# Second layer norm of a decoder layer: root and bias of five row tiles through TensorE instead of VectorE

## The chip, the cores and the metric

The kernel runs on one core of a Trainium2 chip. The metric is device time in microseconds (us) from launch to end; lower is better. The median of the runs shown is 1836.4 us. The profile's clock starts at the first instruction of the span, and all times of rows below are on that clock.

## What is computed

The kernel is a whole decoder layer on 2048 rows of 1024 float32 channels: a mixer of two branches, a first layer norm, a mixture of SwiGLU experts and a second layer norm. Only the end matters here:

```
h   = layer_norm(ALPHA * x + mix, ln1_g, ln1_b)
moe = hier_moe(h, ...)
out = layer_norm(ALPHA * h + moe, ln2_g, ln2_b)

layer_norm(x, g, b): mu = mean(x); var = mean((x - mu)^2)
                     return (x - mu) * rsqrt(var + 1e-5) * g + b
```

## The kernel before

The experts (L1520 to L1553) add their rows into the DRAM tensor `acc`, which also holds ALPHA times h. After the last expert the second norm begins (from L1584). Its 2048 rows are 16 tiles of 128 rows by 1024 channels, grouped in six units `F[k]` of 2, 2, 4, 2, 4 and 2 tiles. A tile is called (k, t) below: (4, 2) is tile 2 of unit 4. SyncE's queue loads every unit from `acc` at L1590, in order.

Four steps make the norm of a unit:

- the moments: for units 1, 2, 4 and 5 on ScalarE (`moments`, L1610), two passes per tile; for units 0 and 3 on VectorE (`moments_v`, L1599).
- `scale1` (L1629): on VectorE, one instruction per tile, f = (f - mean) * g. The vector g lies in PSUM as `g2p`.
- `root` (L1637): on VectorE, rsqrt by a first guess and three Newton steps, 11 small instructions on [128, n] columns named `f_v`, `f_rs` and `f_q`. `f_rs` holds the roots.
- `scale2` (L1651): on VectorE, one instruction per tile, f = f * rs + b, with b in PSUM as `b2p` (L1662). When a pair of tiles, or a tile that stands alone, is done, SyncE's queue stores it to `out` (L1664).

One tile in each of the units 1 to 4, (1, 1), (2, 3), (3, 1) and (4, 3), is left out of `scale1` and `scale2` and normed on GpSimd (POOL) by three instructions of its own once the roots are there: L1657, L1658 and L1659, with g and b in SBUF (`eraw`). It stores that tile itself (L1660).

The order on each engine is the order in which the code is written. `weave` (L1669) takes turns: one step of the next unit's root, one tile of `scale2` of the unit before or of `scale1` of the next. For unit k from 3 on it weaves `scale2(k - 1)` and `scale1(k)` with `root(k)` (L1687). After the last unit's root its two tiles are scaled and stored (L1689). TensorE has no work in the whole second norm; ScalarE's last instruction there is the last pass of unit 5's moments.

Of the kernel before, what the change touches and what calls it, by code (L numbers as in the profile page):

```python
# [10 lines left out]
F32 = mybir.dt.float32  # L11
# [4 lines left out]
AF = mybir.ActivationFunctionType  # L16
OP = mybir.AluOpType
# [68 lines left out]
def layer(ctx, tc, a, out, dbg=None):  # L86
    nc = tc.nc
    A, G, SP = nc.scalar, nc.gpsimd, nc.sync
    V, PE = Clocked(nc.vector, dve_cost), Clocked(nc.tensor, pe_cost)
# [14 lines left out]
    def bigt(shape, dt, name):  # L104
        n = 1
        for d in shape[1:]:
            n *= d
        return big.tile(shape, dt, name=name, tag="big", bufs=NBIG)

    def pmm(shape, name="mm"):  # L110
        return ps.tile(shape, F32, name=name, tag="mm", bufs=4)
# [5 lines left out]
    ident = cst.tile([128, 128], F32, name="ident")  # L117
    make_identity(nc, ident[:])
    ones = cst.tile([128, 128], F32, name="ones")
# [878 lines left out]
    for m, s in order:  # L998
        w = WQ[36 + m]
        gfetch(seq)  # L1000
        p = pmm([128, 512])
# [311 lines left out]
    p = NP - 1  # L1313
# [241 lines left out]
    g2, b2 = [RAW[1][:, 2 * i:2 * i + 2, :].rearrange("p k c -> p (k c)") for i in range(2)]  # L1555
# [5 lines left out]
    with tc.If(mx > 128 * JB):  # L1561
        with tc.For_i(0, NE, 1) as e:
            c = nc.values_load(cnt[0:1, ds(e, 1)], engines=ALL, min_val=0, max_val=S)
# [20 lines left out]
    fp = ctx.enter_context(tc.tile_pool(name="fp", bufs=1, side="right"))  # L1584
    F, i = [], 0
    for n in (2, 2, 4, 2, 4, 2):
        f = bigt([128, n, D], F32, "f")
# [36 lines left out]
    pf = ctx.enter_context(tc.tile_pool(name="pf", bufs=1, space=PSUM))  # L1624
    G2, B2 = [pf.tile([128, D], F32, name=nm) for nm in ("g2p", "b2p")]
# [11 lines left out]
    def root(k):  # L1637
# [5 lines left out]
        for _ in range(3):  # L1643
# [4 lines left out]
            yield  # L1648
            V.scalar_tensor_tensor(rs, q, 1.5, rs, op0=OP.add, op1=OP.mult)

    def scale2(k):  # L1651
        i, n, f = F[k]
        done = 0
        for t in range(n):
            nm, rs = [ST2[k][q][:, t:t + 1] for q in (0, 2)]
            if POOL.get(k) == t:
                G.tensor_scalar(f[:, t], f[:, t], nm, rs, op0=OP.add, op1=OP.mult)  # L1657
                G.tensor_tensor(f[:, t], f[:, t], g2, op=OP.mult)  # L1658
                G.tensor_tensor(f[:, t], f[:, t], b2, op=OP.add)  # L1659
                G.dma_start(out[0, (i + t) * 128:(i + t + 1) * 128, :], f[:, t])  # L1660
                continue
            V.scalar_tensor_tensor(f[:, t], f[:, t], rs, B2, op0=OP.mult, op1=OP.add)  # L1662
            if t - done == 1 or POOL.get(k) == t + 1 or k + 1 == len(F):
                SP.dma_start(out[0, (i + done) * 128:(i + t + 1) * 128, :].rearrange("(t p) d -> p t d", p=128),  # L1664
                             f[:, done:t + 1])
                done = t + 1
            yield
# [12 lines left out]
    moments_v(0)  # L1680
    weave([], root(0))
    weave([scale1(0), scale2(0)], iter(()))
    weave([scale1(1)], root(1))
    weave([scale2(1)], iter(()))
    moments_v(3)
    weave([scale1(2)], root(2))
    for k in range(3, len(F)):  # L1687
        weave([scale2(k - 1), scale1(k)], root(k))
# [25 lines left out]
```

## Time and profile before

| | us |
|---|---|
| median of 3 runs | 1836.4 (1833.97 to 1838.92) |
| the profiled execution, its own time | 1839.48 |
| its span, first to last instruction | 1837.8 |
| what lies around the span | 1.7 |
| TensorE busy in the span | 1702.5 (93%) |
| VectorE busy | 1319.6 (72%) |
| ScalarE busy | 696.7 (38%) |
| mean granted TensorE clock, share of full | 0.968 |

The second norm is the end of the span: the last expert's matmul starts at 1765.1 us, the first tile of `acc` is there at 1778.8 us, and the last instruction ends at 1837.8 us. [...] A timeline row gives start, duration, engine, line, operation, what is written and what is read, shapes and count; its bracket is the idle time of the engine before it and who ended it. Most VectorE and TensorE rows carry L66, the line of a helper, so rows are told apart by their tiles. A matmul's recorded duration contains the way through the array, so it is longer than the distance to the next one.

### The profile page before, as it was taken

How to read it: one execution, taken by the hardware profiler on the slowest of the kernel's cores; microseconds unless marked ns; L12 is line 12 of the kernel's file. 1: busy time of each engine (PE TensorE's matmuls, PEld its weight loads, DVE VectorE, ACT ScalarE, POOL GpSimd, SP SyncE). 2: the span in 40 equal slices, each digit the busy share in tenths (PEclk: the TensorE clock that was granted, in tenths of full speed). 3: DMA queues.
4: the chain of work that ended last, by engine and by line, in shares of the span. 5: the costliest groups of instructions: out<-in, count | busy, mean ns of one | idle time of the engine just before them, and what ended most of it. 6: DMA issues, size and time to landing. Idle time of an engine off the chain costs nothing. (4 is left out here: it accounts for less than half of the span.)

```text
span 1837.8 us, 23924 instructions
## 1 busy us (share of the span) xinstructions
PE 1702.5 (93%) x8368; PEld 1370.4 (75%) x8369; DVE 1319.6 (72%) x2429; ACT 696.7 (38%) x1069; POOL 312.7 (17%) x319
## 2 busy tenths in 40 slices
PE   8999999999999999999999999992999999999930
PEld 6888877777777778788788888871777787777730
DVE  5798787777876875755575768886756656567758
ACT  5111221222222222633330122324766656667754
POOL 2000001101110101000000012122333333333315
PEclk9999999999999999999999999995999999999975
DMA  7321432432342335343464333447788968889855
GB/s 219 93 92 46 117 83 68 150 94 80 104 139 79 101 95 208 94 138 121 162 207 127 115 115 138 161 149 224 243 257 277 288 177 263 261 270 332 247 184 228
DMA packets 214026, 300.81 MB, mean 164 GB/s; under 512 B 29390, under 2 KB 159520, under 8 KB 211312
## 3 DMA queue, kind: packets, MB, share of 16 engines
q1 hardware_dynamic: 166496, 213.32, 35.3%
q0 software_dynamic: 23152, 56.06, 11.2%
q10 hardware_dynamic: 24224, 29.47, 4.8%
q8 instruction: 86, 1.41, 0.3%
q14 instruction: 68, 0.56, 0.1%
HBM read 224.77 MB, written 92.31 MB: 173 GB/s over the span
## 5 line engine op out<-in xcount | busy, mean ns | idle before, releaser
L66 PE MATMUL mm<-xh,whi 128*128 128x512 f32 x896 | 360.8, 403 | 0.0
L66 PE MATMUL mm<-xl,whi 128*128 128x512 f32 x896 | 353.5, 395 | 0.0
L66 PE MATMUL mm<-xh,wlo 128*128 128x512 f32 x896 | 352.2, 393 | 0.0
L66 PE MATMUL pg<-egu,bhl 128*128 128x512 f32 x1176 | 285.2, 398 | 8.3 <-DVEq L1486 6.7
L66 DVE SCALAR_TENSOR_TENSOR cvw<-cvw,cw 128x1024 f32<-128x1024 f32 x240 | 292.0, 1279 | 0.0
L66 PEld LDWEIGHTS pg<-egu,bhl 128*128 128x128 f32 x1176 | 218.5, 189 | 58.2 <-ACT yy L1462 6.5
L66 PEld LDWEIGHTS mm<-xh,whi 128*128 128x128 f32 x896 | 168.3, 188 | 47.9 <-ACT y L712 5.8
L66 PEld LDWEIGHTS mm<-xh,wlo 128*128 128x128 f32 x896 | 168.2, 188 | 41.5
L66 PEld LDWEIGHTS mm<-xl,whi 128*128 128x128 f32 x896 | 168.6, 188 | 36.5 <-DVE xl L66 0.2
L66 PE MATMUL mm<-yt,whi 128*128 128x512 f32 x512 | 163.6, 399 | 2.2 <-ACT yt L858 1.5
L66 PE MATMUL mm<-wo,mh 128*128 128x512 f32 x512 | 164.5, 402 | 0.0
L66 DVE TENSOR_TENSOR egu<-eraw,egu 128x1024 fp32r<-128x1024 f32 x128 | 150.8, 1219 | 15.1 <-ACT egu L1245 12.7
L731 ACT ACTIVATE gt<-mm,cols 128x512 f32<-128x512 f32 x64 | 44.0, 688 | 265.4 <-PE mm L66 260.5
L1245 ACT ACTIVATE egu<-eraw 128x1024 fp32r<-128x1024 f32 x128 | 128.4, 1059 | 8.3 <-DMA td<-r_sd,r_sl 3.3
L66 PE MATMUL pd<-edn,hh 128*128 128x512 f32 x392 | 126.7, 404 | 1.0 <-ACT hh L1447 1.0
L66 PEld LDWEIGHTS mm<-yt,whi 128*128 128x128 f32 x512 | 95.9, 188 | 27.0 <-DVE yt L66 2.5
L66 PEld LDWEIGHTS mm<-wo,mh 128*128 128x128 f32 x512 | 95.6, 191 | 21.9 <-issue 1.2
L66 PE MATMUL mm<-wo,ml 128*128 128x512 f32 x256 | 101.9, 398 | 0.0
L66 PE MATMUL mm<-yt,wlo 128*128 128x512 f32 x256 | 101.0, 395 | 0.0
L66 DVE TENSOR_TENSOR edn<-erd,edn 128x1024 fp32r<-128x1024 f32 x64 | 75.6, 1223 | 26.7 <-ACT edn L1245 25.6
L1206 POOL DMA_INDIRECT td<-r_sd,r_sl x32 | 38.2, 1193 | 312.9 <-DVE r_sl L66 303.4
L1465 POOL DMA_INDIRECT acc<-yy,lq x31 | 49.7, 1603 | 227.9 <-ACT yy L1462 220.7
(300 smaller groups left out, 2558.0 us busy)
## 6 DMA issues: line engine op xcount, KB each, us to landing
eraw<-in_w_gate_dram SPq DMA_DIRECT2D x64, 512.0 KB
eraw<-in_w_up_dram SPq DMA_DIRECT2D x64, 512.0 KB
erd<-in_w_down_dram SPq DMA_DIRECT2D x32, 1024.0 KB
gd<-gt ACTq DMA_DIRECT2D x64, 256.0 KB
gl<-gd SPq DMA_DIRECT2D x64, 256.0 KB
wraw<-in_w_in_dram SPq DMA_DIRECT2D x28, 512.0 KB
xt<-in_x_dram SPq DMA_DIRECT2D x16, 512.0 KB
rg<-in_x_dram SPq DMA_DIRECT2D x8, 1024.0 KB
```

Of the source, the lines that this page charges most:

```text
L66: return f(*args, **kw)
L731: A.activation(gt, p, AF.Sigmoid, bias=cols[:, BI + 12 + m:BI + 13 + m])
L1206: d = G.indirect_dma_start(out=td, out_offset=bass.IndirectOffsetOnAxis(ap=sl[:, t, k:k + 1], axis=0), in_=sd[:, t, k, :], in_offset=None)
L1245: A.activation(h, src, AF.Copy)
L1465: G.indirect_dma_start(out=acc, out_offset=bass.IndirectOffsetOnAxis(ap=idx, axis=0), in_=y, in_offset=None, bounds_check=S - 1, oob_is_er ...
```

## The change

For the five tiles (3, 0), (4, 0), (4, 1), (4, 2) and (5, 0) `scale2` no longer calls VectorE's one instruction. VectorE instead builds a 128 by 128 diagonal matrix of the tile's 128 roots (`f_dg`, two buffers). TensorE multiplies each half of the tile, 128 by 512, by that matrix into a PSUM tile (`f_p`, four buffers) and adds the bias by a second matmul into the same PSUM tile, a column of 128 ones times one row of b. ScalarE copies the half back into the tile in SBUF. All operands are float32. The stores stay where they were in the order of SyncE's queue.

```diff
+    ARRAY = {(3, 0), (4, 0), (4, 1), (4, 2), (5, 0)}
+
+    def through_array(r, rs):
+        dg = fp.tile([128, 128], F32, name="f_dg", bufs=2)
+        V.tensor_scalar(dg, ident, rs, None, op0=OP.mult)
+        for h in range(2):
+            c = slice(512 * h, 512 * h + 512)
+            p = pf.tile([128, 512], F32, name="f_p", bufs=4)
+            PE.matmul(p, dg, r[:, c], start=True, stop=False)
+            PE.matmul(p, ones[0:1, :], b2[0:1, c], start=False, stop=True)
+            A.activation(r[:, c], p, AF.Copy)
+
     def scale2(k):
...
-            V.scalar_tensor_tensor(f[:, t], f[:, t], rs, B2, op0=OP.mult, op1=OP.add)
+            if (k, t) in ARRAY:
+                through_array(f[:, t], rs)
+            else:
+                V.scalar_tensor_tensor(f[:, t], f[:, t], rs, B2, op0=OP.mult, op1=OP.add)
```

On VectorE, from the end of unit 4's root to the end of the kernel (`f_rs` the roots, `f_dg` the diagonal, `f<-f,f_nm,g2p` a tile of `scale1`, `f<-f,f_rs,b2p` a tile of `scale2`), one piece of the difference:

```order
 L66 TENSOR_SCALAR f_v<-f_va 128x2
-L66 SCALAR_TENSOR_TENSOR f<-f,f_rs,b2p 128x1024
+L66 TENSOR_SCALAR f_dg<-ident,f_rs 128x128
 L66 TENSOR_SCALAR f_rs<-f_v 128x2
-L66 SCALAR_TENSOR_TENSOR f<-f,f_rs,b2p 128x1024
+L66 TENSOR_SCALAR f_dg<-ident,f_rs 128x128
 L66 TENSOR_TENSOR f_q<-f_rs 128x2
-L66 SCALAR_TENSOR_TENSOR f<-f,f_rs,b2p 128x1024
+L66 TENSOR_SCALAR f_dg<-ident,f_rs 128x128
 L66 SCALAR_TENSOR_TENSOR f_q<-f_v,f_q 128x2
```

The three tiles of unit 4 that VectorE scaled among the first steps of unit 5's root are now three builds of a diagonal at the same places.

On TensorE, after the branch that ends the expert part (`f_p` the PSUM tile, `eraw` the row of b, `ones` the column of ones), the first of the five tiles, rows of the change alone:

```order
L1561 UNCONDITIONAL_BRANCH
L66 MATMUL f_p<-f,f_dg 128x512
L66 MATMUL f_p<-eraw_9798,ones 128x512
L66 MATMUL f_p<-f,f_dg 128x512
L66 MATMUL f_p<-eraw_9798,ones 128x512
```

Where TensorE's program ended, it now has these four matmuls five times over, in the order of the tiles.

## Rows read from the trace of the kernel before

**Rows 1.** The page's first line, and the last two pieces of the chain that ended last.

```profile
span 1837.8 us, 23924 instructions
...
1831.61 1.28 DVE f L66
1832.89 1.19 DVEq L1710
```

**Rows 2.** Stretches of TensorE: us, busy (instructions), granted clock, DMA share, GB/s.

```profile
1227.30:1229.50 2.20, 0.00 (x0) 1.00 1.09 367
...
1230.30:1236.30 6.00, 6.00 (x15) 0.50 1.01 370
...
1280.93:1284.10 3.17, 3.17 (x11) 0.50 0.20 83
...
1765.50:1768.80 3.30, 0.01 (x1) 1.00 0.13 20
1768.90:1812.00 43.10, 0.00 (x0) 0.50 0.80 297
```

**Rows 3.** VectorE's timeline: unit 3's moments, then units 3 to 5.

```profile
1796.03 2.19 DVE L66 TENSOR_SCALAR f_nm<-f_mv 128x2 f32<-128x2 f32 x1
...
1812.19 1.28 DVE L66 SCALAR_TENSOR_TENSOR f<-f,f_rs,b2p 128x1024 f32<-128x1024 f32 x1
1813.39 0.16 DVE L66 TENSOR_SCALAR f_rs<-f_v 128x4 int32<-128x4 int32 x1
1813.59 2.32 DVE L66 TENSOR_TENSOR f_q<-f_rs 128x4 f32<-128x4 f32 x1
...
1821.68 0.16 DVE L66 SCALAR_TENSOR_TENSOR f_rs<-f_q,f_rs 128x4 f32<-128x4 f32 x1
...
1823.14 1.28 DVE L66 SCALAR_TENSOR_TENSOR f<-f,f_rs,b2p 128x1024 f32<-128x1024 f32 x1
...
1826.77 1.31 DVE L66 SCALAR_TENSOR_TENSOR f_q<-f_v,f_q 128x2 f32<-128x2 f32 x1
```

**Rows 4.** GpSimd's timeline: the last instruction of (1, 1), then (3, 1), (4, 3).

```profile
1795.84 2.36 POOL L1659 TENSOR_TENSOR f<-f,eraw 128x1024 f32<-128x1024 f32 x1
...
1812.27 1.20 POOL L1657 TENSOR_SCALAR f<-f,f_nm,f_rs 128x1024 f32<-128x1024 f32 x1 [1.66 <-DVE f_v L66]
1813.55 2.34 POOL L1658 TENSOR_TENSOR f<-f,eraw 128x1024 f32<-128x1024 f32 x1
...
1822.02 1.19 POOL L1657 TENSOR_SCALAR f<-f,f_nm,f_rs 128x1024 f32<-128x1024 f32 x1 [2.82 <-DVE f_v L66]
1823.29 2.35 POOL L1658 TENSOR_TENSOR f<-f,eraw 128x1024 f32<-128x1024 f32 x1
```

**Rows 5.** VectorE's groups by form: one TENSOR_SCALAR of 128 by 1024 in SBUF.

```profile
L66 DVE TENSOR_SCALAR cvw<-cvw,cw,cols 128x1024 f32<-128x1024 f32 x8 | 6.2, 810 | 9.8 <-DMA cd<-cvw 9.5 <-DMA cvw<-vd 0.4
```

**Rows 6.** TensorE's timeline at the full clock, around one float32 matmul of the convolution's norm.

```profile
727.36 1.02 PE L66 MATMUL aux<-nw,onesm 128*128 128x512 f32 x2
...
728.44 0.40 PE L66 MATMUL mm<-xl,whi 128*128 128x512 f32 x1
728.68 0.39 PE L66 MATMUL mm<-xh,wlo 128*128 128x512 f32 x1
```

**Rows 7.** TensorE's timeline at half the clock, the output projection.

```profile
1232.16 1.05 PE L66 MATMUL mm<-wo,mh 128*128 128x512 f32 x2
...
1233.44 1.05 PE L66 MATMUL mm<-wo,mh 128*128 128x512 f32 x2
```

**Rows 8.** TensorE's groups by form: float32 matmuls of 128 and of 64 contracted rows.

```profile
L66 PE MATMUL aux<-utl,M 128*128 128x128 f32 x192 | 24.0, 275 | 0.0
...
L66 PE MATMUL aux<-sx,CA 64*128 64x128 f32 x256 | 18.6, 285 | 0.0
```

**Rows 9.** ScalarE's timeline: a 128 by 512 copy out of PSUM.

```profile
1765.55 0.69 ACT L1462 ACTIVATE yy<-pd,ll 128x512 f32<-128x512 f32 x1 [0.64 <-PE pd L66]
```

**Rows 10.** The end of the span by stretch: us, granted clock, DMA share, GB/s.

```profile
1833.70:1836.30 2.60, 0.50 0.99 402
```

## The prediction

> **What bounds the kernel now.** I read the page's first line and the chain that ended last, then TensorE by stretch, then the timelines of VectorE and GpSimd (POOL) from unit 3 on. The chain shows what ends the span: VectorE's last two tiles, (5, 0) done at 1832.89 and (5, 1) 1.19 us later, and behind them the stores [rows 1]. From (5, 0) done to the end of the span are 1837.8 - 1832.9 = 4.9 us, in which the data of both stores run for 2.6 us without a gap at 402 GB/s [rows 10], which is their 1.05 MB. So VectorE is on the path, and a faster VectorE would shorten it. TensorE is not: it has stood still since 1765.5, its clock fell at 1768.8, and at 1812 it is still at the lower of its two levels [rows 2].
>
> The two timelines show why VectorE takes as long as it does. Whenever GpSimd works on its tile, some of VectorE's smallest instructions last as long as GpSimd's running one: `f_q` from 1813.59 for 2.32 us, to 1815.91, where GpSimd's instruction from 1813.55 ends at 1815.89 [rows 3, 4]; `f_nm`, a TENSOR_SCALAR, from 1796.03 to 1798.22, where GpSimd's ends at 1798.20 [rows 3, 4]; `f_q` again at 1826.77 for 1.31 us [rows 3]. The big instructions that read one operand from PSUM are not held: the `scale2` tile at 1823.14 takes its 1.28 us beside GpSimd's instruction of 1823.29 [rows 3, 4].
>
> **The change, part by part.** *VectorE.* Five instructions go. From one start to the next such a tile takes 1813.39 - 1812.19 = 1.20 us [rows 3], so 6.0 us go. Five builds of a diagonal come. No row has a TENSOR_SCALAR of 128 columns; one of 1024 takes 0.81 us [rows 5] and one of 4 takes 0.16 [rows 3], which puts 128 at about 0.24, 1.2 us for five, if nothing holds them. The lower end is 0.16, the upper end 2.19, the TENSOR_SCALAR that GpSimd held [rows 3]. On paper VectorE gains 4.8 us.
>
> In unit 3 I book none of it. Behind the removed tile (3, 0) stand the first guess of the root and then the `f_q` that waits for GpSimd until 1815.91 anyway [rows 3]; reaching it 0.95 us sooner only waits longer. So unit 4's root ends where it did, at 1821.68 + 0.16 = 1821.84 [rows 3], or at most 1.15 us sooner if that wait is not what it seems. In unit 4 the three tiles that ran undisturbed beside GpSimd are replaced by an instruction of the kind that was held. GpSimd has two seams between its three instructions, and in the trace one held instruction passes at a seam. The first guess of unit 5's root takes one, the diagonal of (4, 1) the other (about 1826.0), and `f_q`, which had the first seam before, is left until GpSimd is done at about 1828.3. The rest of unit 5's root then ends about 1 us later than before, and the diagonal of (5, 0) is there at about 1833.1; unheld it would be there by 1830.
>
> [...]
>
> *TensorE.* Per tile come four float32 matmuls of 128 by 512. The trace has such a matmul, recorded as two instructions: from its start to the start of the matmul after the next are 728.44 - 727.36 = 1.08 us, of which one ordinary matmul is 728.68 - 728.44 = 0.24, so 0.84 us at the full clock [rows 6]. A tile is 4 x 0.84 = 3.4 us, against the 1.2 us that it took on VectorE. At the lower level it is twice that, 6.7 us; the ordinary matmul has three in 1.28 us there against three in 0.72 [rows 6, 7], 1.8 times, and I take 2, as the granted clock is half. For the second matmul, with one contracted row, no row has a price: with 64 rows, two of which share the array, one instruction costs 18.6/256 = 73 ns against 24.0/192 = 125 ns with 128 rows [rows 8], 0.6 of the price. I take the whole price, since its neighbours on the engine use all rows and nothing can share the array with it; 0.6 and less is a rival.
>
> [...]
>
> *The clock.* In this trace it fell 2.2 us after TensorE stopped at 1227.3 and 3.3 us after it stopped at 1765.5; it rose 3.2 us after work began at 1280.93 and 6.0 us after it began at 1230.3 [rows 2]. (3, 0) begins at about 1812.19 + 0.24 + 0.3 = 1812.7 (0.3 for the signal, which took GpSimd 1822.02 - 1821.84 = 0.18 [rows 3, 4], and for loading the weights), at the lower level. With 1.6 to 3.0 us lost to it, it ends at 1817.7 to 1819.1. (4, 0) cannot begin before 1821.84 + 0.24 + 0.3 = 1822.4. That is 3.3 to 4.7 us of rest, and both falls came within 3.3. So I expect (4, 0) to begin at the lower level again.
>
> *ScalarE and the stores.* Ten copies of 0.69 us [rows 9] on an engine that has nothing else left; nine lie beside matmuls and only the last is on the path. SyncE's stores wait for ScalarE in the old order; (5, 1) from VectorE is done before (5, 0) and waits behind it. With both released together, the data still take their 2.6 us, so the 4.9 us at the end stand.
>
> *The sum.* (4, 0), (4, 1), (4, 2) and (5, 0) run one behind the other, because each tile takes TensorE longer than its diagonal is late (1826.0, about 1829 and 1833.1, against tile ends not before 1827.4, 1830.8 and 1834.1). Start 1822.4, four tiles 13.4, lost to the clock half of 3.2 to 6.0, in the middle 2.3: 1838.1. The way out of the array 0.15 (0.39 recorded less 0.24 [rows 6]), the signal and ScalarE's copy 0.75: 1839.0. The end as before, 4.9: 1843.9. Against the span of 1837.8 that is **6.1 us more**. The profiled execution's own time, 1839.48, is 3.1 above the median of the three runs, 1836.4; I put the difference on the median: 1842.5. Its ends: unit 4's root 1.15 sooner and the clock up after 3.2 give 4.2 more; the clock up after 6.0 and (4, 0)'s diagonal held behind GpSimd's first instruction, 1.2 us [rows 4], give 8.0 more.
>
> **The rivals.** Three tenths of a per cent, about what a measurement of this kernel can tell from no change, are 5.5 us.
>
> *Not slower: TensorE keeps the clock between (3, 0) and (4, 0).* If the hold in unit 3 goes with the removed tile, (4, 0) begins at about 1821.2; if (3, 0) ends as late as 1819.1, the rest is 2.1 us, under the shortest fall of 2.2. That is where it decides. Then four tiles at full clock end at 1834.6, the span at 1840.4: 2.6 more, 1839.0. If the clock stays but VectorE is held, (5, 0) waits for its diagonal at 1833.1 and the span ends at 1842.6: 4.8 more, 1841.2. Against it: the second fall came only after 3.3, but the rest is likely longer than that too.
>
> *The bias matmul is cheap.* At half its price a tile is 2.5 us. TensorE is then no longer the only bound: (5, 0) starts with its diagonal at 1833.4 and the span ends at 1841.7: 3.9 more, 1840.3. For it speak the rows with 64, against it that those had a partner.
>
> *The clock stays low.* Half of the new matmuls have one contracted row, and no row shows whether such work lifts the clock. Four tiles at 6.7 end at 1849.3 and the span at 1855.1: 17.3 more, 1853.7.
>
> Even the first two together, VectorE unheld, the clock kept and the bias cheap, leave (5, 0) waiting for its diagonal: 1830 + 0.3 + 2.5 + 5.8 (array, copy and end) = 1838.6, 0.8 more. A gain of 5.5 us has no mechanism; only scatter of the runs (1833.97 to 1838.92) can give it.
>
> **How the numbers follow.** Forecast 0.51, the clock kept 0.22, a cheap bias 0.12, the clock low 0.12, scatter 0.03. Of the forecast, 4.2 to 8.0 more, I put 0.41 above 5.5 and 0.10 below. Slower: 0.41 + 0.12 = 0.53. Same: 0.10 + 0.22 + 0.12 = 0.44. Faster: 0.03. The predicted time is the forecast's 1842.5. The range runs from the clock kept, 1839.0 less half a us of scatter, to the forecast's upper end, 1844.4 and some scatter: 1838.5 to 1846.0. Outside lie the low clock, the gain, and some 0.05 at the ends. The forecast alone is 1840.6 to 1844.4.
>
> **What would show it.** In the new trace: the chain should end in TensorE `f_p`, ScalarE L1662, store, no longer VectorE. TensorE's `f_p` rows should show four tiles without a gap from about 1822, the clock at 0.50 at the first and 1.00 some 3 to 6 us later. The diagonals that meet a GpSimd instruction should last over 1 us. The forecast is wrong if TensorE waits for diagonals, if the bias rows come closer than 0.8 us apart at the full clock, or if the clock is at one level throughout.

## The result and the profile after

The changed kernel takes 1858.61 us (median of 4 runs, 1857.93 to 1859.66) against 1836.37 (4 runs, 1833.97 to 1838.92): a ratio of 1.0121, with a 95% interval of 1.0107 to 1.0134. That is 22 us more. The forecast was 6.1 us more and ended its range at 1846.0, so the direction was right and the size was not.

Runs of one kernel scatter by some 2.5 us to either side, and much of it lies ahead of the second norm: in the profiles below, whose edits all lie in that norm, VectorE's first `f_bs` instruction starts anywhere from 1774.6 to 1781.6 us. To compare single profiles I therefore use the norm's own time, from VectorE's first `f_bs` instruction to the end of the span: 1837.8 - 1778.8 = 59.0 us before, 1856.3 - 1776.4 = 79.9 us after. One kernel profiled twice gave 57.9 and 58.2 us (e4 and e11 below). Below, "norm + 42" is 42 us behind that start.

The page's first line and the chain that ended last, the changed kernel (to be held against [rows 1]; columns: start, us, engine, tile, line):

```profile
span 1856.3 us, 24032 instructions
...
1818.02 0.16 DVE f_rs L66
1818.18 0.08 DVE f_v L66
1818.27 0.25 DVE f_dg L66
1818.52 0.04 issue
1818.56 32.13 PE f_p L66 x32
...
1850.72 0.60 ACT f L1662
```

The end has moved from VectorE to TensorE, as forecast. From the root of unit 4 on there is one piece of 32.13 us: the 32 recorded instructions of four tiles, (4, 0) to (5, 0), without a gap, 8.03 us a tile. The forecast had 13.4 us for them, and 2.3 for the clock.

Stretches of TensorE in the changed kernel (us, busy (instructions) of PE, PEld, DVE, ACT, POOL, granted clock, DMA share, GB/s): tile (3, 0), the other four tiles, and the tail, against [rows 2] and [rows 10]:

```profile
1810.50:1818.50 8.00, 7.76 (x8) 1.67 (x7) 7.83 (x16) 0.80 (x2) 5.98 (x5) 0.50 0.14 59
1818.56:1850.70 32.14, 32.12 (x32) 7.99 (x32) 6.28 (x16) 4.51 (x8) 6.38 (x4) 0.50 0.21 83
1851.30:1856.30 5.00, 0.00 (x0) 0.00 (x0) 0.00 (x0) 0.02 (x1) 0.00 (x0) 0.50 0.52 210
```

The granted clock is 0.50 from the first product to the last: 40 us in which TensorE was busy but for the 0.3 us ahead of (4, 0), and the clock never rose. In [rows 2] it rose 3.2 and 6.0 us after work began.

TensorE's timeline of the changed kernel, the first three products of tile (4, 0). A product is one float32 matmul of the code, recorded as two instructions (x2); the operand that TensorE loads before it, here the diagonal or the ones, is called its weights:

```profile
1818.56 2.07 PE L66 MATMUL f_p<-f,f_dg 128*128 128x512 f32 x2 [0.30 <-DVE f_dg L66]
1820.57 2.07 PE L66 MATMUL f_p<-eraw,ones 1*128 1x512 f32 x2
1822.57 2.08 PE L66 MATMUL f_p<-f,f_dg 128*128 128x512 f32 x2
```

The weight loads (PEld) in the same stretch:

```profile
1818.56 0.50 PEld L66 LDWEIGHTS f_p<-f,f_dg 128*128 128x128 f32 x2 [1.88 <-DVE f_dg L66]
1820.57 0.50 PEld L66 LDWEIGHTS f_p<-eraw,ones 1*128 1x128 f32 x2 [1.50 <-issue]
1822.57 0.50 PEld L66 LDWEIGHTS f_p<-f,f_dg 128*128 128x128 f32 x2 [1.50 <-issue]
```

A product takes 2.0 us from start to start, not the 1.68 (twice 0.84) of the forecast. The second view shows where the time goes: each load begins with its matmul, at 1820.57 and 1822.57, and not while the matmul before it still runs. So a load lies on TensorE's path at every product (e14 shows the other case, loads that are ahead). A one-row product costs as much as a full one: 2.00 us from 1820.57 to 1822.57, 2.01 for the one before it.

### The profile page after: what moved, and what is told of

Same layout as the page of the kernel before. It is cut to its first block, busy times and chain, and to the rows that moved or that the text cites. A ratio compares the mean times of both kernels' runs of the same rounds, so it can differ in the third digit from the quotient of the medians.

```text
span 1856.3 us, 24032 instructions
## 1 busy us (share of the span) xinstructions
PE 1740.9 (94%) x8408; PEld 1380.0 (74%) x8409; DVE 1312.5 (71%) x2429; ACT 702.0 (38%) x1079; POOL 312.4 (17%) x319
```

## Experiments

Each kernel is the changed one with the edit shown, unless it says otherwise. The theories began as A (the one-row bias products keep the clock low), B (the zeros of the diagonal do) and C (the loads that are not ahead leave TensorE's array idle 0.3 us in every 2.0, and that does).

**e1: the bias with 128 contracted rows.** `b2` holds b in every row, so the identity times `b2` is the same bias.

```diff
-            PE.matmul(p, ones[0:1, :], b2[0:1, c], start=False, stop=True)
+            PE.matmul(p, ident, b2[:, c], start=False, stop=True)
```

> The bias product takes 128 contracted rows (identity times the bias, which lies on all partitions) instead of one; everything else as in the change. Theory A (matmuls with one contracted row do not lift TensorE's clock, and they were half of the stream): the clock goes to 1.00 within 3 to 7 us of the first f_p matmul, a tile falls from 8.0 to about 3.4 us, and the stretch from the start of (4, 0) to the last ScalarE copy falls from 32.8 to 15 to 18 us. Theory B (zeros: a diagonal matrix moves little through the array): the identity is as empty as the diagonal, so the clock stays at 0.50 and the stretch at 32 to 33 us. Theory C (the weight loads, which are not hidden behind the matmul before, leave the array idle 0.3 us in every 2.0): the same 0.50 and 32 to 33 us.

TensorE's timeline, e1:

```profile
1813.28 2.05 PE L66 MATMUL f_p<-f,f_dg 128*128 128x512 f32 x2 [46.44 <-DVE f_rs L66]
1815.12 1.78 PE L66 MATMUL f_p<-eraw,ident 128*128 128x512 f32 x2
1816.74 1.02 PE L66 MATMUL f_p<-f,f_dg 128*128 128x512 f32 x2
...
1821.65 1.13 PE L66 MATMUL f_p<-f,f_dg 128*128 128x512 f32 x2 [3.03 <-DVE f_dg L66]
1822.61 1.02 PE L66 MATMUL f_p<-eraw,ident 128*128 128x512 f32 x2
...
1834.63 1.02 PE L66 MATMUL f_p<-eraw,ident 128*128 128x512 f32 x2
```

The clock rose 3.4 us after the first product, and stayed at 1.00 through the rest of 3.03 us ahead of (4, 0) and to the end. A product takes 0.86 us, a tile 3.43; the norm takes 61.8 us. With the same number of products, 18.1 of the 20.9 us are gone. From the start of (4, 0) to the end of the last copy it takes 14.6 us, a little less than theory A's 15 to 18. B falls already here, as the identity is as empty as the diagonal. C expected no rise either, but took the loads to stay where they were; in this run the second product begins 1.84 us behind the first and not 2.0, and in e13, whose products are the same, the load for the product of 1820.74 begins at 1820.31, ahead of it. So whether such gaps keep the clock low stays open. Of the forecast's prices, 0.84 a product and 3.4 a tile stand.

**e2: no bias product at all** (five tiles lack their bias).

```diff
-            PE.matmul(p, dg, r[:, c], start=True, stop=False)
-            PE.matmul(p, ones[0:1, :], b2[0:1, c], start=False, stop=True)
+            PE.matmul(p, dg, r[:, c], start=True, stop=True)
```

> The bias product is left out, so the five tiles lack the bias: two float32 matmuls per tile are left, all with 128 rows. Theory A: the clock rises, a tile takes about 1.7 to 2 us after the rise. Theories B and C: the clock stays at 0.50, a tile takes half of 8.0, 4.0 us, and the four tiles at the end 16 us if none waits for its diagonal.

The norm takes 59.9 us. The clock rose 4.0 us after the first product, 0.3 us behind the end of (3, 0)'s products, fell in the rest of 4.62 us ahead of (4, 0) and rose again 5.9 us after (4, 0) began. The same diagonal products got the clock with the one-row products between them gone.

**e3: a full matrix for the diagonal** (the five tiles hold scaled sums).

```diff
-        V.tensor_scalar(dg, ident, rs, None, op0=OP.mult)
+        V.tensor_scalar(dg, ones, rs, None, op0=OP.mult)
```

> The 128 by 128 matrix is full (ones times the roots) instead of diagonal, so the five tiles hold sums instead of scaled rows; instructions, shapes and waits are those of the change, the bias product with its one row too. Theory B (zeros): the clock rises and a tile falls below 5 us. Theories A and C: 0.50 throughout, 8.0 us per tile, the same end of the span as the change within 1 us of the start of the norm.

79.9 us for the norm, 0.50 throughout and 2.0 us a product, as the change. The zeros make no difference here; theory B falls for good.

**e5: 128 rows in (3, 0), one row in the other four tiles.**

```diff
+            if first:
+                PE.matmul(p, ident, b2[:, c], start=False, stop=True)
+            else:
+                PE.matmul(p, ones[0:1, :], b2[0:1, c], start=False, stop=True)
...
-                through_array(f[:, t], rs)
+                through_array(f[:, t], rs, k == 3)
```

> Tile (3, 0) adds its bias with 128 contracted rows, as in the run with 128 rows for all five; the four later tiles keep the one row of the change. In the run with 128 rows the clock was at 1.00 from the middle of (3, 0) on and through the 3 us of rest. Theory A (a stream half of whose matmuls have one row neither lifts the clock nor keeps it): the four tiles begin at 1.00 or fall to 0.50 soon after (4, 0) has begun, and then go at 8.0 us a tile; the norm, from its first bn_stats to the last instruction, takes over 74 us. Rival (such a stream does not lift the clock, but keeps it): 1.00 to the end and about 62 us. The stretch at 1.00, if there is one, shows what a one-row matmul costs at the full clock: 0.86 us as one with 128 rows, less (0.5 or so), or more, if its weights are not loaded ahead.

TensorE's timeline, e5, from the start of (4, 0):

```profile
1819.10 1.13 PE L66 MATMUL f_p<-f,f_dg 128*128 128x512 f32 x2 [2.49 <-DVE f_dg L66]
1820.16 1.12 PE L66 MATMUL f_p<-eraw,ones 1*128 1x512 f32 x2
...
1825.42 2.08 PE L66 MATMUL f_p<-f,f_dg 128*128 128x512 f32 x2
1827.43 2.07 PE L66 MATMUL f_p<-eraw,ones 1*128 1x512 f32 x2
```

(4, 0) began at 1.00. There an alternating product takes 1.05 us, 0.2 more than in e1. The clock fell to 0.50 at 1825.4, while TensorE worked without a gap, and stayed there: 74.2 us. A rest of 2.49 us lies ahead of this stream; e1's 128-row products kept the clock behind a longer one. So the alternating stream did not lift the clock in the change (0.50 for 40 us) and did not keep it in this run.

**e12: the products grouped**, both diagonal ones of a tile first, then both one-row ones.

```diff
+        c = [slice(512 * h, 512 * h + 512) for h in range(2)]
+        p = [pf.tile([128, 512], F32, name="f_p", bufs=4) for h in range(2)]
         for h in range(2):
-            c = slice(512 * h, 512 * h + 512)
-            p = pf.tile([128, 512], F32, name="f_p", bufs=4)
-            PE.matmul(p, dg, r[:, c], start=True, stop=False)
-            PE.matmul(p, ones[0:1, :], b2[0:1, c], start=False, stop=True)
-            A.activation(r[:, c], p, AF.Copy)
+            PE.matmul(p[h], dg, r[:, c[h]], start=True, stop=False)
+        for h in range(2):
+            PE.matmul(p[h], ones[0:1, :], b2[0:1, c[h]], start=False, stop=True)
+            A.activation(r[:, c[h]], p[h], AF.Copy)
```

> The change, but in each tile both diagonal products first and then both one-row products, so that TensorE goes from 128 rows to one and back once in a tile, not twice. Theory 'exposed loads by the switch, low clock by the one-row products themselves': the granted clock stays at 0.50, each matmul behind one of its own kind takes 1.7 us and not 2.0, a tile 7.4 us for 8.03, the norm some 77 us (79.9 in the change). Rival 'the gaps at the exposed loads keep the clock low': it rises in the first or second tile and the norm takes 62 to 70 us. Rival 'every one-row product has its load exposed, whatever stands ahead': 8.03 us a tile and 79.9 us as in the change.

TensorE's timeline, e12, from its first product:

```profile
1810.45 3.75 PE L66 MATMUL f_p<-f,f_dg 128*128 128x512 f32 x4 [46.59 <-DVE f_rs L66]
1814.13 3.78 PE L66 MATMUL f_p<-eraw,ones 1*128 1x512 f32 x4
1818.81 3.71 PE L66 MATMUL f_p<-f,f_dg 128*128 128x512 f32 x4 [0.90 <-DVE f_dg L66]
1822.44 1.98 PE L66 MATMUL f_p<-eraw,ones 1*128 1x512 f32 x4
```

The same, by stretch:

```profile
1810.45:1822.00 11.55, 10.65 (x12) 3.47 (x12) 9.30 (x17) 1.19 (x2) 9.44 (x6) 0.50 0.22 91
1822.50:1836.00 13.50, 13.39 (x29) 4.62 (x28) 7.17 (x13) 4.25 (x8) 2.85 (x2) 1.00 0.39 157
```

A tile at half clock takes 7.46 us, as the first theory had it: two exposed loads fewer. But against that theory the clock rose, 11.6 to 12.1 us after the first product, and stayed: 65.3 us. Half of these products still contract one row. So theory A in its plain form falls: in this run one-row products, half of all, did not keep the clock low. What is left is the gap at each exposed load, the switch, or how long 128-row products run without a one-row product between them: 3.7 us here against 2.0 in the change, and the rise came some 3.5 us into the second such run.

**e13: larger gaps in a stream of 128 rows.** e1 with one `f_p` buffer, so that each pair of products waits for ScalarE's copy.

```diff
-            p = pf.tile([128, 512], F32, name="f_p", bufs=4)
+            p = pf.tile([128, 512], F32, name="f_p", bufs=1)
```

> The change with the bias by the 128-row identity, and one PSUM buffer f_p for four: each pair of products now waits until ScalarE has copied the pair before it, a rest of about 0.9 us (0.60 the copy and the two hand-overs) behind 3.4 us of work at half clock. That leaves TensorE idle for a larger share (0.9 of 4.3 us) than the exposed loads of the change do (0.3 of 2.0). Theory 'the alternation of 128 rows and one': no such alternation here, so the clock rises to 1.00 in the first or second tile, a tile takes about 5.3 us, the norm 67 to 71 us. Rival 'gaps between the products, whatever makes them': 0.50 to the end, 8.6 us a tile, the norm 80 to 84 us.

TensorE's timeline, e13, around the second rise of the clock:

```profile
1827.45 2.07 PE L66 MATMUL f_p<-f,f_dg 128*128 128x512 f32 x2 [0.69 <-ACT f L1662]
1829.32 1.91 PE L66 MATMUL f_p<-eraw,ident 128*128 128x512 f32 x2
1831.92 1.13 PE L66 MATMUL f_p<-f,f_dg 128*128 128x512 f32 x2 [0.69 <-ACT f L1662]
1832.88 1.02 PE L66 MATMUL f_p<-eraw,ident 128*128 128x512 f32 x2
1834.59 1.13 PE L66 MATMUL f_p<-f,f_dg 128*128 128x512 f32 x2 [0.69 <-ACT f L1662]
```

The clock rose 2.9 us after the first product, fell at 1821.1, 1.3 us into the work behind a rest of 2.36 us, rose again at 1831.4 and stayed at 1.00 although TensorE rested 0.69 of every 2.67 us. The norm takes 72.7 us, 1.7 above what I expected, for the fall in between. At half clock it rested 0.69 of every 4.47 us there, the same share as the change's 0.3 in 2.0 for an exposed load. So gaps of that share did not keep the clock low here either; they come half as often, though, once in two products.

**e14 and e15: 96 and 32 rows** (the five tiles lack the bias in their other rows).

```diff
-            PE.matmul(p, ones[0:1, :], b2[0:1, c], start=False, stop=True)
+            PE.matmul(p, ident[0:96, :], b2[0:96, c], start=False, stop=True)
```

> The change with the bias by the identity's first 96 rows against 96 rows of b2 (rows 96 to 127 of the five tiles get no bias, which leaves the time as it is). If any switch of the row count exposes the load: 2.0 us a product, clock 0.50, the norm about 79.9 us as in the change. If only a product that uses few of the array's rows does: loads ahead, the clock rises some 3.4 us after the first work, the norm 61 to 63 us as with 128 rows.

> The same with the identity's first 32 rows (rows 32 to 127 of the five tiles get no bias). If what one row costs is the switch to a small part of the array: as the change, 2.0 us a product, 0.50 to the end, about 79.9 us. If it is the single row itself: loads ahead and 61 to 63 us as with 128 rows.

TensorE's timeline, e14, from (4, 0) on:

```profile
1820.57 2.08 PE L66 MATMUL f_p<-f,f_dg 128*128 128x512 f32 x2 [2.57 <-DVE f_dg L66]
1822.44 1.92 PE L66 MATMUL f_p<-eraw,ident 96*128 96x512 f32 x2
1824.14 1.91 PE L66 MATMUL f_p<-f,f_dg 128*128 128x512 f32 x2
1825.85 1.47 PE L66 MATMUL f_p<-eraw,ident 96*128 96x512 f32 x2
1827.15 1.02 PE L66 MATMUL f_p<-f,f_dg 128*128 128x512 f32 x2
```

Its weight loads, of the second product above and of the third:

```profile
1822.44 0.34 PEld L66 LDWEIGHTS f_p<-eraw,ident 96*128 96x128 f32 x1 [0.52 <-issue]
1823.29 0.34 PEld L66 LDWEIGHTS f_p<-f,f_dg 128*128 128x128 f32 x1 [0.52 <-issue]
```

TensorE's timeline, e15:

```profile
1818.74 2.08 PE L66 MATMUL f_p<-f,f_dg 128*128 128x512 f32 x2 [0.30 <-DVE f_dg L66]
1820.74 2.07 PE L66 MATMUL f_p<-eraw,ident 32*128 32x512 f32 x2
1822.74 2.08 PE L66 MATMUL f_p<-f,f_dg 128*128 128x512 f32 x2
```

With 96 rows the loads are ahead (the one for the product of 1824.14 begins at 1823.29; 1.70 us a product at half clock, 0.86 at full) and the clock rises. With 32 rows all is as in the change: 2.0 us a product, 0.50 to the end, 79.9 us. So a single row did nothing that 32 did not. e14 took 65.5 us, 2.5 above what I expected: its clock fell at 1819.9, in a rest of 2.57 us ahead of (4, 0), and came back 6.1 us after (4, 0) began. e1 had kept it through 3.03 us.

**e4: only (3, 0) through the array** (one-row bias).

```diff
-    ARRAY = {(3, 0), (4, 0), (4, 1), (4, 2), (5, 0)}
+    ARRAY = {(3, 0)}
```

> Only tile (3, 0) goes through TensorE, the other four stay on VectorE. On the change's trace VectorE ended unit 4's root 1.2 us earlier, counted from the first bn_stats of the norm (41.8 us against 43.0). If that comes from (3, 0) alone, the norm from its first bn_stats to the last instruction is 1.2 us shorter than before (59.0 us), so 57.8; if the earlier forecast held (GpSimd's hold eats it), it is 59.0. TensorE's 8.0 us for the tile end by about 45 us into the norm and are not on the path.

57.9 us, 1.1 less than before. The tile takes its 8 us on a TensorE that nobody waits for, and VectorE saves a tile in unit 3: unit 4's root ends at norm + 41.9, as in the change. **e11** is the same kernel, timed:

> The kernel with (3,0) alone on the array, bias by one row, as run once before at 57.9 us for the norm and 1834.5 us, now timed in rounds. If the 1.1 us is real and no scatter: 1.0 to 1.5 us less than the kernel before (ratio 0.9992 to 0.9994). Rival 'it was the scatter of one run': a ratio of 0.9997 to 1.0005.

The ratio is 0.9995 (0.9986 to 1.0004; 11 runs against 21 of the kernel before) and its profile again shows less, 58.2 us. A gain of this size can't be told from none by these runs.

**e6: (5, 0) back on VectorE**, 128-row bias, four diagonal buffers.

```diff
-    ARRAY = {(3, 0), (4, 0), (4, 1), (4, 2), (5, 0)}
+    ARRAY = {(3, 0), (4, 0), (4, 1), (4, 2)}
...
-        dg = fp.tile([128, 128], F32, name="f_dg", bufs=2)
+        dg = fp.tile([128, 128], F32, name="f_dg", bufs=4)
```

> Bias with 128 rows, a diagonal buffer for each tile, and (5, 0) back on VectorE. If VectorE in unit 5's root is bound by GpSimd's hold and not by its own tiles, taking (4, 0) to (4, 2) from it gives nothing beyond the run with (3, 0) alone: the norm takes 57.9 us, within 0.4. If VectorE's tiles count, it is up to 2.9 us (three tiles of 1.2 less 0.24 each) shorter, 55.0.

**e7: GpSimd's tile of unit 4 given to VectorE too**, with three tiles through the array, the 128-row bias and three diagonal buffers; **e8: the same POOL line without the array** (`ARRAY` empty).

```diff
-    POOL = {1: 1, 2: 3, 3: 1, 4: 3}
+    POOL = {1: 1, 2: 3, 3: 1}
...
-    ARRAY = {(3, 0), (4, 0), (4, 1), (4, 2), (5, 0)}
+    ARRAY = {(3, 0), (4, 0), (4, 1)}
```

> Bias with 128 rows, (3, 0), (4, 0) and (4, 1) through TensorE, and unit 4's tile (4, 3) taken from GpSimd and given to VectorE, so that nothing holds VectorE from there on. If GpSimd's hold is what eats VectorE's gain, the norm falls to about 56.4 us (1.4 below the run with (3, 0) alone); if not, it stays at 57.9 or rises by the 2.4 us of (4, 3)'s two instructions.

> The kernel before with (4, 3) on VectorE instead of GpSimd and no tile through TensorE: tells what of the run before this one is the array's. By VectorE's durations the norm takes 59.0 to 59.6 us: 2.4 us of work more, 2.0 to 2.4 us of holds less.

e8 took 58.8 us, 0.2 below what I expected. e6 took 60.7 and e7 62.9, both over 2 us above the highest that I expected, although all work was done early: in e7 VectorE ended at norm + 51.9 and ScalarE's last copy at norm + 52.8. The tail was 10 us long instead of 5. Stretches of e7, the last column GB/s:

```profile
1820.00:1825.00 5.00, 4.01 (x6) 1.77 (x7) 4.86 (x15) 0.29 (x1) 0.00 (x0) 0.66 0.26 105
1825.00:1831.00 6.00, 4.82 (x12) 1.83 (x10) 4.47 (x9) 2.09 (x4) 0.00 (x0) 1.00 0.00 0
1831.00:1839.10 8.10, 0.00 (x0) 0.00 (x0) 0.00 (x0) 0.00 (x0) 0.00 (x0) 0.73 0.98 387
```

For 6 us nothing moved, while VectorE finished tile after tile; then 3.1 MB went at once. SyncE's queue issued four stores from 1830.5 to 1832.5, directly behind ScalarE's last copy (1829.86 + 0.60): the store of (4, 0) and (4, 1) waited for that copy, and VectorE's finished tiles stood behind it. What SyncE's queue waited for in e7 (us in total, times, the longest):

```profile
SPq L1680 <- ACT f L1662: 20.0, 2, 11.2
```

**e9: e7 with the array tiles' stores on ScalarE's queue**, and unit 4's other tiles stored one by one; **e10: e6 with the first edit alone.**

```diff
                 through_array(f[:, t], rs)
+                A.dma_start(out[0, (i + t) * 128:(i + t + 1) * 128, :], f[:, t])
+                done = t + 1
+                yield
+                continue
...
-            if t - done == 1 or POOL.get(k) == t + 1 or k + 1 == len(F):
+            if t - done == 1 or POOL.get(k) == t + 1 or k > 3:
```

> The kernel without GpSimd in unit 4 (array tiles (3,0), (4,0), (4,1), 128-row bias), and beside it the array tiles' stores issued one by one from ScalarE's queue behind their copies, the vector tiles of unit 4 stored one by one from SyncE's. Theory 'blocked queue': there VectorE was done 51.9 us and ScalarE 52.8 us behind the norm's start, but no byte was stored from 1820 to 1831, since VectorE's finished tiles stood in SyncE's queue behind a store that waited for ScalarE; so the stores now spread and the norm takes 57 to 58.5 us (62.9 there, 59.0 in the kernel before), the program 0.5 to 2 us less than before. Rival 'the transfers are slow by themselves or the copies end it': the norm stays at 61 to 63 us, the program 2 to 5 us slower than before.

> The kernel with four array tiles ((5,0) back on VectorE, 128-row bias, four diagonal buffers), its array tiles' stores now issued one by one from ScalarE's queue. 'Blocked queue': it ended its vector work at 52.8 us and its copies at 53.4 us behind the norm's start and still took 60.7 us; with the stores apart 57.5 to 58.8 us. Rival 'not the queue': 60 to 61 us as there.

e9 took 59.3 us (e7 62.9), e10 58.8 (e6 60.7). The queue it was. e10 came in at the upper end of what I expected and e9 above it: its last three stores were issued within 2 us, their data moved at some 400 GB/s until 1832.2, 2.8 us behind the end of the last copy, and the span ended another 3.6 us later, for which no cause is shown. Timed, e9 is at 0.9996 (0.9987 to 1.0005): no version that I tried beats the kernel before measurably.

## Why the prediction was wrong, point by point

*Right: what bounds it.* VectorE's removed tiles, 1.20 us each, buy less than TensorE's take, 8.03 each, and the chain ends in `f_p`, the copy, the store.

*Wrong, and the cause of the miss: the clock.* The step that failed is the rise of the clock, 3.2 to 6.0 us into the work: "lost to the clock half of 3.2 to 6.0, in the middle 2.3". It took the two rises of [rows 2] for what any work on TensorE would meet; both came under products that contract 128 rows, the slower one under those of [rows 7]. The work of this change doesn't: alternating 128 rows and one, the clock stayed at 0.50 for 40 us, "at one level throughout", which the prediction had named as a sign of being wrong. "I expect (4, 0) to begin at the lower level again" came true by luck: the clock had not fallen in a rest, it had never risen in (3, 0), and the rest was 0.30 us. The rival "the clock stays low" named that, with 0.12; its reason, that no row showed whether such work lifts the clock, deserved more weight than the forecast's 0.51 left it. Its price, 1853.7, was low as well, for the next reason.

*Wrong: the price at half clock.* "At the lower level it is twice that, 6.7" left out that the loads were not ahead where the row count jumped between 128 and 1 (the change) or 32 (e15): 2.0 us a product, where 96 rows (e14) took 1.7, and 8.03 for 6.8 us a tile. The doubling itself was right (1.70 for 0.86); the rows behind it, [rows 6] and [rows 7], show neighbours that all contract 128 rows.

The two in sum: four tiles at half clock, loads hidden, are 16 x 1.70 = 27.2 us against 13.4 + 2.3 forecast, 11.5 more; the exposed loads add 32.1 - 27.2 = 4.9. With the start 1.4 earlier (norm + 42.2 for 43.6) and the copy 0.3 shorter than booked, 65.1 + 11.5 + 4.9 - 1.7 = 79.8, and 79.9 was measured.

*The rest of the forecast holds where the clock does.* In the norm's time it was 65.1 us. e14, whose clock fell ahead of (4, 0) and rose 6.1 us into it, took 65.5, in part because errors cancel: (4, 0) began 1.3 us earlier than forecast, the four tiles took 1.2 longer and the stretch behind them 0.5. e1, where the clock lasted through the rest, is the rival "TensorE keeps the clock": 2.6 more forecast, 2.8 measured. Behind such a rest the clock went either way: it fell within rests of 2.57 and 4.62 us (e14, e2), 1.9 and 3.7 us after the work ended, and 1.3 us after one of 2.36 (e13); it lasted through 2.49 and 3.03 (e5, e1). So the 2.2 us at which that rival let it be decided decided nothing.

*Wrong, small: "In unit 3 I book none of it."* VectorE's timeline of the changed kernel, against [rows 3]:

```profile
1810.11 0.96 DVE L66 TENSOR_TENSOR f_q<-f_rs 128x4 f32<-128x4 f32 x1
...
1814.62 1.31 DVE L66 SCALAR_TENSOR_TENSOR f_rs<-f_q,f_rs 128x4 f32<-128x4 f32 x1
...
1824.68 0.29 DVE L66 TENSOR_SCALAR f_dg<-ident,f_rs 128x128 f32<-128x128 f32 x1 [5.00 <-PE f_p L66]
...
1832.69 0.29 DVE L66 TENSOR_SCALAR f_dg<-ident,f_rs 128x128 f32<-128x128 f32 x1 [4.16 <-PE f_p L66]
```

GpSimd's timeline, the changed kernel, against [rows 4]:

```profile
1809.79 1.28 POOL L1670 TENSOR_SCALAR f<-f,f_nm,f_rs 128x1024 f32<-128x1024 f32 x1 [1.67 <-DVE f_v L66]
```

`f_q` is held until 1811.07 (1809.79 + 1.28), the end of GpSimd's first instruction, not its second. With the tile gone it arrives one instruction earlier, and each step behind it does so too: `f_rs`, free before, now meets GpSimd's third instruction (1.31 us), and one tile of `scale1` fewer is left to do behind that. Unit 4's root ends at norm + 41.8 instead of + 43.0. The 1.15 that I kept for the range's end is close to the 1.2 that came, and e4 shows that (3, 0) alone gives it. So the early start that the first rival needs, which the forecast did not book, is what came: (4, 0) began at norm + 42.2, and that rival had 42.4.

*Not met here, and without effect: the held builds.* None of the five was held, each took 0.28 or 0.29 us; the fourth and fifth waited for a buffer that TensorE had not released, 5.00 and 4.16 us, which the forecast had left out. VectorE was done at 1834.2, 16 us before TensorE. But none of the five met one of GpSimd's two longer instructions: the third began 0.13 us into the short first one, and when the fourth had its buffer, GpSimd was done. Where the fourth did meet one it was held, as forecast: for 0.75 us in e1, 2.24 in e2. VectorE and GpSimd in e1:

```profile
1824.53 0.75 DVE L66 TENSOR_SCALAR f_dg<-ident,f_rs 128x128 f32<-128x128 f32 x1 [1.76 <-PE f_p L66]
1822.85 2.35 POOL L1671 TENSOR_TENSOR f<-f,eraw 128x1024 f32<-128x1024 f32 x1
```

*Right, and less general than I put it: the stores.* The tail is 5.0 us (4.9 forecast), as TensorE comes last. Where the array's tiles end earlier, e6 and e7, the old order on SyncE's queue cost 1.9 us (e6 60.7, e10 58.8) and 3.6 us (e7 62.9, e9 59.3).

*Right, and on the low side: the whole price for the one-row product.* Against the rival "the bias matmul is cheap", no one-row product came out below a full one: 1.05 us at the full clock in e5 against e1's 0.86, 2.0 at half clock in the change against 1.70 in e14, and the 128-row products beside it cost as much. The 64-row instructions of [rows 8], which spoke for that rival, begin two at a time: from 565.16 to 565.96 us in the trace of the kernel before the number of them under way goes from 4 to 6 and back, against 2 to 3 with 128 rows from 563.62 to 564.30.

*Open.* That the one-row product is the cause of both losses is shown (61.8 and 65.5 us in e1 and e14, 79.9 in the change and e15); how the clock stays low under it is not. Neither half of the products having one row (e12, 1.00 from 12 us on) nor gaps (e13, 1.00 at the end) did it alone; under the alternation at every product, with 1 or 32 rows, the clock was 0.50 to the end (the change, e3, e15). Whether it is the two together, the longer run of 128-row products that e12 also brings, or something in the switch itself was not separated. Each of these runs was profiled once.

## What to carry to other kernels

Before work is moved to an idle TensorE, price it at the clock that this very stream will get, not at the clock that other work in the kernel got, and look whether its neighbours have the same number of contracted rows. Here the bias as a 128-row product with an identity got 1.00 after 3.4 us, the one-row product 0.50 for 40 us, and the norm took 18 us less with the first (61.8 for 79.9), though still 2.8 us more than before the change. If operands must differ, group the products of a kind: that took the norm from 79.9 to 65.3 us here (e12). And when a tile's last step moves to another engine, move its store to a queue where nothing finished earlier stands behind it: 3.6 us here in e9, 1.9 in e10.

## What the runs showed that I had not expected

- TensorE lost the clock while it was busy without a gap: in e5 it fell from 1.00 to 0.50 at 1825.4, 6.3 us into a stream of alternating products with no rest in it (2.49 us of rest lie ahead of the stream).
- A product of 32 rows (e15) and one of a single row (the change), alternating with 128, cost the same 2.0 us at half clock; one of 96 rows (e14) cost 1.70, as the 128-row one behind it, 1.71.
- Of the five tiles taken from VectorE the one in unit 3 gave 1.2 us at the root of unit 4 by itself (e4), because the steps behind it met GpSimd's instructions one earlier.
